# Two of the merge's sixteen column chunks projected among the last two heads of the first attention

## The chip, the cores and the metric

The kernel runs on one core of a Trainium2 chip. The metric is the device time of one execution in microseconds (us). The core has a matrix engine, TensorE (PE in the profile, its weight loads PEld), and four others: VectorE (DVE), ScalarE (ACT), GpSimd (POOL) and SyncE (SP). Each runs its own list of instructions in a fixed order; they meet at semaphores. DMA queues move data between the chip's memory and the core's own.

## What is computed

The reference is two transformer blocks. The change lies in the first attention part of the first one, for 512 tokens of width 1024. Of it this matters:

```python
z = u @ w_in[layer]
q_a, kc, vc, ksl, vsl, kwn, vwn, g_a, q_b, k_b, v_b, m_a, m_b = jnp.split(z, split_at, axis=-1)
...
y_a = nsa_attention(q_a, k_cmp, v_cmp, k_slc, vsl.reshape(kv_shape), k_win, vwn.reshape(kv_shape), g_nsa, rel_bias) @ w_up_nsa[layer]
y_b = stick_breaking_attention(q_b.reshape(sb_shape), k_b.reshape(sb_shape), v_b.reshape(sb_shape)) @ w_up_sb[layer]
mixed = (jax.nn.sigmoid(m_a) * y_a + jax.nn.sigmoid(m_b) * y_b) @ w_out[layer]
```

There are eight softmax heads (`nsa_attention`) and eight stick-breaking heads. `m_a` and `m_b` are 1024 columns of `u @ w_in` each and are needed only in the last line, the merge.

## The kernel before

`attention1` lays out the first attention part. Activations stand transposed, features on the 128 partitions and the 512 tokens along the free dimension. It projects keys, values and queries of the softmax heads, runs the eight `nsa_head` generators, then projects q, k and v of the stick-breaking heads and runs the eight `sb_head` generators; `merge1` follows.

A matrix product in full precision is made of three: weights and activations are split into a high part and a rest (line 117: ScalarE copies the high part, VectorE subtracts it), and `mm3` (lines 127 to 129) multiplies high by high, high by rest and rest by high. `gemm` loops it over the eight blocks of 128 input features, so a chunk of 128 output columns of `w_in` is 24 matmuls of 128x128 weights against 512 tokens, into a PSUM bank of the tag G, of which there are two.

`m_a` and `m_b` are columns 2840 to 4888 of `w_in`, 16 chunks, numbered 0 to 15. `project` loads 256 columns at a time, splits them and calls `gemm` for each chunk; `take_m` copies the bank with VectorE (line 1079). Chunks 0, 1 and 8 stay in the core in a tile `sg`; the other thirteen go through a tile `mo` of two buffers and a DMA that POOL issues (line 1083) into the array `md` in the chip's memory, from which `merge1` reads them back. The pool of `mo` opens when the pools of the softmax heads close and takes their space, so a copy into `mo` waits until these heads have ended.

A softmax head computes the scores against the 32 compressed keys (`Sc`, eight small matmuls, line 666) and against two sets of keys (line 693), each row's minimum and sum (VectorE, line 695, ScalarE, line 697), turns the probabilities with the matmul's transpose (line 536), splits them (line 170) and multiplies them by the values into one bank O (lines 544 and 546). `in_turn` starts a head while the one before it is still at its values. A stick-breaking head (lines 745 to 790) makes score products, an exponential and a logarithm on ScalarE (lines 761 to 763), a maximum and a split on VectorE (lines 764, 765) and POOL (line 766), sums over later keys with triangular and all-ones matmuls (lines 769 and 775), and multiplies by the values (line 788).

The order on each engine is not the order in which the program is written. A scheduler simulates the program when it is built and gives each engine's free time to instructions that could go then; earlier code has precedence, later code fills. The merge's chunks depend on nothing but `u` and the weights, so their matmuls fill TensorE's gaps among the heads, as far as banks and weight buffers are free. This order is fixed in the program.

Of the kernel before, what the change touches and what calls it, by code (L numbers as in the profile page):

```python
# [9 lines left out]
F32 = mybir.dt.float32  # L10
# [37 lines left out]
class Tiles:  # L48

    def __init__(self, tiles, n):  # L50
        self.tiles, self.n = tiles, n
# [21 lines left out]
class Kernel:  # L73
    def __init__(self, tc, a, out):
        self.tc, self.nc, self.a, self.out = tc, tc.nc, a, out
        self.exps, self.split_after = [], []

    def pool(self, name, side="left"):
        return self.tc.tile_pool(name=name, bufs=1, side=side, reuse_waits="tile")
# [574 lines left out]
    def nsa_head(self, h, qn, kd, vs, kdc, vsc, gates, parts, wk):  # L654

        nc = self.nc
        r0, g = 64 * (h % 2), h // 4
        QS = wk.tile([128, 512], F32R, name="QS", bufs=2)
        self.stack(QS, qn[:, h // 2], r0)
        band = self.band(h, wk)  # L660

        Sc = self.ps("S", 3)
        for r in range(4):
            qb = 3 - r
            for i in range(2):
                nc.tensor.matmul(Sc[:, r * 32:r * 32 + 32], QS[:, qb * 128:(qb + 1) * 128], kdc[i][:, g],
                                 start=(i == 0), stop=(i == 1))
        xc = wk.tile([128, 4, 32], F32, name="xc", bufs=2)
        nc.vector.memset(xc[:, :, 31:32], BIG)
        bv = band[:, 31:896]  # L670
        b3 = bass.AP(tensor=bv.tensor, offset=bv.offset, ap=[list(bv.ap[0]), [128, 4], [16, 31]])
        nc.vector.tensor_add(xc[:, :, :31], Sc[:, :128].rearrange("p (r c) -> p r c", r=4)[:, :, :31], b3)
        st = wk.tile([128, 4, 8], F32, name="st", bufs=2)
        nc.vector.tensor_reduce(st[:, 0, 0:4], xc[:, :, :31], axis=AX.X, op=OP.min)
        ec = wk.tile([128, 4, 32], F32, name="ec", bufs=2)
        nc.vector.tensor_sub(ec, xc, st[:, 0, 0:4].unsqueeze(2).to_broadcast([128, 4, 32]))
        nc.scalar.activation(ec, ec, AF.Exp, scale=-1.0)
        nc.vector.tensor_reduce(st[:, 1, 0:4], ec[:, :, :31], axis=AX.X, op=OP.add)
        nc.vector.tensor_scalar(st[:, 1, 0:4], st[:, 1, 0:4], 1e-30, None, op0=OP.max)
        nc.vector.reciprocal(st[:, 1, 0:4], st[:, 1, 0:4])  # L680
        nc.vector.tensor_mul(st[:, 1, 0:4], st[:, 1, 0:4], gates[:, 3, :, h])
        nc.vector.tensor_mul(ec[:, :, :31], ec[:, :, :31], st[:, 1, 0:4].unsqueeze(2).to_broadcast([128, 4, 31]))
        Ps = []
        for b in range(2):
            P = wk.tile([128, 1280], F32, name="P", bufs=3)
            Ps.append(P)
            mn, sm = st[:, 2, 4 * b:4 * b + 4], st[:, 3, 4 * b:4 * b + 4]
            for qb in range(4):
                n = (qb + 1) * 128
                x = P[:, ROW[qb]:ROW[qb] + n]  # L690
                ps = self.ps("S", 3)
                for i in range(2):
                    nc.tensor.matmul(ps[:, :n], QS[:, qb * 128:(qb + 1) * 128], kd[b][i][:, :n],
                                     start=(i == 0), stop=(i == 1))
                nc.vector.tensor_tensor_reduce(x, ps[:, :n], band[:, 384 - qb * 128:512], 1.0, 3e38,
                                               OP.add, OP.min, mn[:, qb:qb + 1])
                nc.scalar.activation(x, x, AF.Exp, bias=mn[:, qb:qb + 1], scale=-1.0, accum_out=sm[:, qb:qb + 1])
            yield
        Tc = self.ps("T", 2)
        for r in range(4):  # L700
            nc.tensor.transpose(Tc[:32, (3 - r) * 128:(4 - r) * 128], ec[:, r], self.ident)
        C = wk.tile([32, 512], F32, name="C", bufs=1)
        nc.scalar.activation(C, Tc[:32], AF.Copy)
        O = self.ps("O", 1)
        nc.tensor.matmul(O, vsc[:, g], C, start=True, stop=False, skip_group_check=True)
        for b in range(2):
            P, sm = Ps[b], st[:, 3, 4 * b:4 * b + 4]
            nc.vector.tensor_scalar(sm, sm, 1e-30, None, op0=OP.max)
            nc.vector.reciprocal(sm, sm)
            nc.vector.tensor_mul(sm, sm, gates[:, 1 + b, :, h])  # L710
            for qb in range(4):
                self.scale_rows(qb, P, sm)
            self.transposed_values(O, lambda j: vs[b][:, j, g], P, wk, False, b == 1)
            if b == 0:
                yield
        self.heads_parts(h, O, parts, self.np)
# [110 lines left out]
                self.gemm(ps, self.parts(w[:, :, m:m + 128]), [x[:, :, at] for x in act])  # L827
                consume((s + m) // 128, ps)

    def project(self, u, name, c0, n, consume, k0=0, first=None, k=8, early=(), banks=()):  # L830

        step = 2048 // k // 128 * 128
        done = 128 * len(early)
        if early:
            w = [self.load(self.w_cols(name, c0 + s, step, k0, k)) for s in range(0, done, step)]
            v = [self.parts(w[i // 2][:, :, i % 2 * 128:i % 2 * 128 + 128], place) for i, place in enumerate(early)]
            self.split_after = [self.normed]
            ps = [self.ps("S", 3) if i > 1 else self.ps("G", 2) for i in range(len(v))]  # L840
            for at in HALVES:
                for i, (x, y) in enumerate(zip(ps, v)):
                    self.gemm(x[:, at], y, [z[:, :, at] for z in u], after=self.behind_ms if i == 2 else None)
            for i, x in enumerate(ps):
                consume(i, x)
                self.step()
        for s in range(done // step * step, n, step):
            if s >= done:
                w = first[0] if first and s == 0 else self.load(self.w_cols(name, c0 + s, min(step, n - s), k0, k))
            else:  # L850
                w = w[-1]
            whole = self.parts(w) if k == 1 else None
            for m in range(max(0, done - s), min(step, n - s), 128):
                ps = self.ps(*banks[(s + m) // 128]) if (s + m) // 128 < len(banks) else self.ps("G", 2)
                e = min(m + 128, n - s)
                if whole:
                    v = [x[:, :, m:e] for x in whole]
                else:
                    v = first[1][m // 128] if first and first[1] and s == 0 else self.parts(w[:, :, m:e])
                self.gemm(ps[:e - m], v, u)  # L860
                consume((s + m) // 128, ps)
                self.step()

# [124 lines left out]
    def attention1(self, u, md, first, dram):  # L988

        nc = self.nc  # L990
# [5 lines left out]
        with self.pool("nsap") as sp:  # L996
# [4 lines left out]
            with self.pool("nsa0") as wk:  # L1001
# [36 lines left out]
                kdc, vsc = self.compress(sp, wk, kg[:, 0:1])  # L1038
# [13 lines left out]
            def keep(dst, scale):  # L1052
                def f(m, ps):
                    nc.scalar.activation(dst[:, m], ps, AF.Copy, scale=scale)
                return f
# [5 lines left out]
            self.project(u, "w_in", 1304, 512, keep(qT, 0.125))  # L1061
            self.project(u, "w_in", 1816, 512, keep(kT, 1.0))
            self.project_rows(u, "w_in", 2328, 512, take_vb)
        with self.pool("mo") as mw:
            self.sg = sbq.enter_context(self.pool("sg", "right"))
            with self.pool("sbw") as wk:

                self.in_turn([self.sb_head(h, qT, kT, vT, places.take, wk) for h in range(8)])


            self.kept = {}

            def take_m(first):
                def f(m, ps):
                    m += first
                    stay = m in (0, 1, 8)
                    t = self.sg.tile([128, 512], F32, name="sg", bufs=3) if stay else \
                        mw.tile([128, 512], F32, name="mo", bufs=2)
                    nc.vector.tensor_copy(t, ps)
                    if stay:  # L1080
                        self.kept[m] = t
                    else:
                        nc.gpsimd.dma_start(md[:, m * 512:(m + 1) * 512], t)
                return f

            for m, n in ((2, 6), (10, 6), (0, 2), (8, 2)):
                self.project(u, "w_in", 2840 + m * 128, n * 128, take_m(m))
        return places_a.new, places.new

# [912 lines left out]
```

## Time and profile before

| what | us |
|---|---|
| median of 3 runs (1799.74 to 1805.24) | 1800.09 |
| the profiled execution, its own time | 1800.61 |
| its span, from the first to the last instruction | 1798.9 |
| TensorE busy | 1719.1 (96%) |
| VectorE busy | 1393.7 (77%) |
| ScalarE busy | 1147.7 (64%) |
| POOL busy | 471.3 (26%) |

Busy times overlap, and an engine's busy share is a mean over stretches with different limits; the change touches the stretch from 228 to 457 us of the span. In a timeline, a bracket at the end of a row is the time in which the engine had nothing to run before that instruction and what ended the wait. The ends of matmuls are modelled and overlap the next one, so their cost is read from start to start. The granted clock is TensorE's, as a share of 2.4 GHz.

### The profile page before, as it was taken

How to read it: one execution, taken by the hardware profiler on the slowest of the kernel's cores; microseconds unless marked ns; L12 is line 12 of the kernel's file. 1: busy time of each engine (PE TensorE's matmuls, PEld its weight loads, DVE VectorE, ACT ScalarE, POOL GpSimd, SP SyncE). 2: the span in 40 equal slices, each digit the busy share in tenths (PEclk: the TensorE clock that was granted, in tenths of full speed). 3: DMA queues.
4: the chain of work that ended last, by engine and by line, in shares of the span. 5: the costliest groups of instructions: out<-in, count | busy, mean ns of one | idle time of the engine just before them, and what ended most of it. 6: DMA issues, size and time to landing. Idle time of an engine off the chain costs nothing. (4 is left out here: it accounts for less than half of the span.)

```text
span 1798.9 us, 24837 instructions
## 1 busy us (share of the span) xinstructions
PE 1719.1 (96%) x8944; PEld 1410.8 (78%) x8944; DVE 1393.7 (77%) x2022; ACT 1147.7 (64%) x1809; POOL 471.3 (26%) x433
## 2 busy tenths in 40 slices
PE   6899998999999999999999999969999999999996
PEld 2678976787898888888979888757777777777774
DVE  4758788888687474747765867879999989999997
ACT  3646676665565343435555666558888878888886
POOL 2204325435133333333312410221212112121113
PEclk9999999999999999999999999979999999999998
DMA  9634113315555656564522214679999999999954
GB/s 326 188 94 137 52 59 125 116 65 192 186 164 183 212 168 211 167 207 153 158 83 83 71 48 176 222 242 343 361 357 359 337 328 385 373 366 368 372 191 168
DMA packets 234400, 377.71 MB, mean 210 GB/s; under 512 B 11817, under 2 KB 102565, under 8 KB 234272
## 3 DMA queue, kind: packets, MB, share of 16 engines
q1 hardware_dynamic: 222752, 345.60, 56.1%
q0 software_dynamic: 11520, 30.47, 5.5%
q8 instruction: 72, 1.18, 0.3%
q14 instruction: 56, 0.46, 0.1%
HBM read 366.64 MB, written 20.73 MB: 215 GB/s over the span
## 5 line engine op out<-in xcount | busy, mean ns | idle before, releaser
L117 ACT ACTIVATE w<-raw 128x1024 fp32r<-128x1024 f32 (+2 forms) x350 | 353.5, 1017 | 296.1 <-PE G L128 226.7
L117 DVE TENSOR_TENSOR w<-raw,w 128x1024 fp32r<-128x1024 f32 (+2 forms) x350 | 422.1, 1225 | 114.4 <-ACT w L117 112.5
L127 PE MATMUL G<-u,w 128*128 128x512 f32 (+1 forms) x688 | 267.8, 390 | 7.7 <-ACT w L117 5.5
L128 PE MATMUL G<-u,w 128*128 128x512 f32 (+1 forms) x688 | 266.2, 387 | 0.4 <-DVE u L229 0.4
L129 PE MATMUL G<-u,w 128*128 128x512 f32 (+1 forms) x688 | 265.8, 387 | 0.1
L127 PE MATMUL S<-w,x 128*128 128x512 f32 x504 | 198.0, 398 | 6.4 <-PEq L1828 3.5
L128 PE MATMUL S<-w,x 128*128 128x512 f32 x504 | 202.7, 402 | 0.0
L129 PE MATMUL S<-w,x 128*128 128x512 f32 x504 | 199.9, 397 | 0.1
L117 DVE TENSOR_TENSOR w<-rawa,w 128x1024 fp32r<-128x1024 f32 x122 | 151.1, 1271 | 19.0 <-ACT w L117 19.0
L127 PEld LDWEIGHTS G<-u,w 128*128 128x128 f32 x688 | 130.6, 190 | 36.5 <-ACT w L117 6.2
L129 PEld LDWEIGHTS G<-u,w 128*128 128x128 f32 x688 | 130.8, 190 | 26.7 <-DVE w L117 2.1
L128 PEld LDWEIGHTS G<-u,w 128*128 128x128 f32 x688 | 131.0, 190 | 25.6 <-DVE u L229 1.0
L117 ACT ACTIVATE w<-rawa 128x1024 fp32r<-128x1024 f32 x122 | 127.9, 1060 | 35.7 <-PE S L129 21.9
L405 POOL TENSOR_TENSOR acc<-acc,araw 128x512 f32<-128x512 f32 x60 | 88.1, 1486 | 238.0 <-ACT araw L403 237.8
L127 PEld LDWEIGHTS S<-w,x 128*128 128x128 f32 x504 | 95.6, 190 | 29.7 <-issue 3.9
L129 PEld LDWEIGHTS S<-w,x 128*128 128x128 f32 x504 | 95.7, 190 | 22.2 <-POOL x L1683 0.9
L128 PEld LDWEIGHTS S<-w,x 128*128 128x128 f32 x504 | 95.8, 190 | 21.1
L128 PE MATMUL G<-hid,w 128*128 128x512 f32 (+1 forms) x320 | 111.1, 347 | 1.2 <-DVE hid L1120 1.2
L129 PE MATMUL G<-hid,w 128*128 128x512 f32 (+1 forms) x320 | 111.3, 348 | 0.0
L127 PE MATMUL G<-hid,w 128*128 128x512 f32 (+1 forms) x320 | 110.9, 347 | 0.0
L1683 POOL TENSOR_TENSOR x<-xg,x 128x512 fp32r<-128x512 f32 x32 | 47.5, 1486 | 228.2 <-ACT x L1682 228.2
L128 PE MATMUL G<-w,hh 128*128 128x512 f32 x248 | 100.8, 407 | 0.0
(637 smaller groups left out, 4021.7 us busy)
## 6 DMA issues: line engine op xcount, KB each, us to landing
raw<-in_mlp_w_dram SPq DMA_DIRECT2D x36, 1024.0 KB, 5.4
raw<-in_w_in_dram SPq DMA_DIRECT2D x33, 1024.0 KB, 5.3
raw<-in_w_expert_up_dram SPq DMA_DIRECT2D x28, 1024.0 KB, 10.0
raw<-in_w_expert_gate_dram SPq DMA_DIRECT2D x27, 1024.0 KB, 9.7
raw<-in_w_expert_down_dram SPq DMA_DIRECT2D x27, 1024.0 KB, 8.8
araw<-in_w_ada_dram SPq DMA_DIRECT2D x96, 256.0 KB, 3.6
rawa<-in_w_expert_gate_dram SPq DMA_DIRECT2D x21, 1024.0 KB, 10.9
rawa<-in_w_expert_up_dram SPq DMA_DIRECT2D x20, 1024.0 KB, 8.8
```

The source lines that it names most:

```text
L117: ins = nc.scalar.activation(r[0], v, AF.Copy), nc.vector.tensor_sub(r[1], v, r[0])
L127: first = nc.tensor.matmul(ps, lhs[0], rhs[0], start=start, stop=False)
L128: nc.tensor.matmul(ps, lhs[0], rhs[1], start=False, stop=False)
L129: self.behind = nc.tensor.matmul(ps, lhs[1], rhs[0], start=False, stop=stop)
L405: nc.gpsimd.tensor_add(x, x, raw)
L1683: nc.gpsimd.tensor_sub(x[1][:, s], y[:, s], x[0][:, s])
```

## The change

The last matmul of each softmax head's compressed scores is kept in a list, `marks`. While the softmax heads' pools are still open, chunks 2 and 3 are projected with a new consumer, `take_early`, which copies the bank into a tile `rstd` of the pool `np` (one buffer) and sends it to `md`. The first matmul of chunk 2 is ordered behind the mark of head 6, that of chunk 3 behind the mark of head 7. The later loop over the chunks begins with chunk 4 instead of chunk 2.

```diff
@@ nsa_head @@
             for i in range(2):
-                nc.tensor.matmul(Sc[:, r * 32:r * 32 + 32], QS[:, qb * 128:(qb + 1) * 128], kdc[i][:, g],
-                                 start=(i == 0), stop=(i == 1))
+                ins = nc.tensor.matmul(Sc[:, r * 32:r * 32 + 32], QS[:, qb * 128:(qb + 1) * 128], kdc[i][:, g],
+                                       start=(i == 0), stop=(i == 1))
+        self.marks.append(ins)
@@ project @@
-                self.gemm(ps[:e - m], v, u)
+                self.gemm(ps[:e - m], v, u, after=behind[(s + m) // 128] if behind else None)
@@ attention1 @@
+            def take_early(m, ps):
+                t = self.np.tile([128, 512], F32, name="rstd", bufs=1)
+                nc.vector.tensor_copy(t, ps)
+                nc.gpsimd.dma_start(md[:, (m + 2) * 512:(m + 3) * 512], t)
+
+
+            self.project(u, "w_in", 2840 + 256, 256, take_early, behind=self.marks[6:8])
         with self.pool("mo") as mw:
...
-            for m, n in ((2, 6), (10, 6), (0, 2), (8, 2)):
+            for m, n in ((4, 4), (10, 6), (0, 2), (8, 2)):
                 self.project(u, "w_in", 2840 + m * 128, n * 128, take_m(m))
```

The new order follows from the scheduler. In the rows below, `G<-u,w` is a chunk's matmul, `O<-P,vs` a value product of a softmax head, `T<-ident,P` a transpose, `O<-P,V` a value product of a stick-breaking head and `neg_tri`, `neg_ones_r` its sums over later keys; the numbers in names tell tiles apart. The lines of after are one higher from the mark on.

TensorE at head 6's second half, where its values meet the first set of probabilities; before:

```order
L536 MATMUL T<-ident,P 128x128 x4
L705 MATMUL O<-C,vsc 128x512
L544 MATMUL O<-P_2139,vs_624 128x512
L546 MATMUL O<-P_2140,vs_624 128x512
L544 MATMUL O<-P_2150,vs_624 128x384
L536 MATMUL T<-ident,P 128x128 x2
L546 MATMUL O<-P_2151,vs_624 128x384
```

and after, up to the first of the chunk matmuls that now stand there:

```order
L544 MATMUL O<-P_2139,vs_624 128x512
L536 MATMUL T<-ident,P 128x128 x2
L546 MATMUL O<-P_2140,vs_624 128x512
L536 MATMUL T<-ident,P 128x128 x3
L127 MATMUL G<-u_164,w_3851 128x512
L128 MATMUL G<-u_165,w_3851 128x512
L129 MATMUL G<-u_164,w_3852 128x512
```

Before, head 6's value products of 512 and 384 tokens follow each other directly; after, 21 chunk matmuls stand between them, the last of 72 behind head 7's mark.

VectorE at head 6's score reductions (ISA rows), before:

```order
L170 TENSOR_TENSOR P_1924<-T,P_1923 128x256
L682 TENSOR_TENSOR ec<-ec,st 128x4x31
L695 ISA P,st<-S,band 128x256
L695 ISA st 128x1
L695 ISA P,st<-S,band 128x384
L695 ISA st 128x1
L117 TENSOR_TENSOR w_3905<-raw,w_3904 128x1024
L695 ISA P,st<-S,band 128x512
```

and after:

```order
L170 TENSOR_TENSOR P_1913<-T,P_1912 128x512
L170 TENSOR_TENSOR P_1924<-T,P_1923 128x256
L696 ISA P,st<-S,band 128x384
L696 ISA st 128x1
L1068 COPY rstd<-G 128x512
L696 ISA P,st<-S,band 128x512
L696 ISA st 128x1
L117 TENSOR_TENSOR w_3852<-raw,w_3851 128x1024
```

The copy of chunk 2 out of its bank (line 1068) now stands between two score reductions, and the split of weights in this place is that of a later load.

TensorE in stick-breaking head 5, before:

```order
L127 MATMUL G<-u_164,w_4299 128x512
L128 MATMUL G<-u_165,w_4299 128x512
L129 MATMUL G<-u_164,w_4300 128x512
L788 MATMUL O<-P_3550,V 128x384
L788 MATMUL O<-P_3549,V 128x128
L788 MATMUL O<-P_3550,V 128x128
L769 MATMUL S<-s_3519,neg_tri 128x256
L775 MATMUL S<-s_3519,neg_ones_r 128x256
L775 MATMUL T<-s_3519,neg_ones_r 128x256
```

and after:

```order
L770 MATMUL T<-s_3600,neg_tri 128x512
L776 MATMUL T<-s_3599,neg_ones_r 128x384
L789 MATMUL O<-P_3629,V 128x384
L770 MATMUL S<-s_3599,neg_tri 128x256
L789 MATMUL O<-P_3630,V 128x384
L789 MATMUL O<-P_3629,V 128x128
L789 MATMUL O<-P_3630,V 128x128
L770 MATMUL S<-s_3600,neg_tri 128x384
L770 MATMUL S<-s_3599,neg_tri 128x128
```

Before, chunk matmuls stand between the head's value products; after, none is left from here to the end of the heads.

## Rows read from the trace of the kernel before

**Rows 1.** Span and mean granted TensorE clock of the core.

```profile
core 0: 1798.9 us, clock 0.983
```

**Rows 2.** Windows by stretch: start:end, length; busy us per engine (instructions); granted clock; DMA.

```profile
228.50:244.40 15.90, 15.90 (x91) 13.03 (x89) 11.04 (x28) 10.16 (x24) 1.97 (x3) 1.00 0.31 89
244.40:257.20 12.80, 12.61 (x78) 10.44 (x77) 12.39 (x43) 8.94 (x25) 4.86 (x8) 1.00 0.23 77
257.20:265.40 8.20, 7.67 (x47) 5.94 (x47) 7.75 (x31) 7.48 (x20) 1.88 (x4) 1.00 0.00 0
265.40:284.20 18.80, 14.99 (x87) 11.08 (x85) 12.64 (x31) 9.05 (x22) 3.79 (x6) 0.94 0.01 1
284.20:292.30 8.10, 8.06 (x26) 6.47 (x27) 7.98 (x8) 6.29 (x12) 7.22 (x6) 0.73 0.62 199
292.30:329.40 37.10, 33.26 (x159) 26.24 (x158) 34.01 (x41) 23.86 (x43) 22.36 (x18) 0.95 0.53 169
329.40:390.00 60.60, 59.22 (x319) 49.91 (x318) 49.95 (x75) 39.41 (x74) 23.06 (x22) 1.00 0.24 79
390.00:429.20 39.20, 38.57 (x207) 32.09 (x206) 31.54 (x55) 23.05 (x44) 17.40 (x16) 1.00 0.32 92
429.20:457.00 27.80, 23.82 (x102) 18.78 (x102) 22.52 (x29) 13.11 (x23) 14.40 (x20) 0.94 0.90 312
```

**Rows 3.** Windows by stretch, TensorE on tile G alone; same columns.

```profile
228.50:244.40 15.90, 9.28 (x36) 1.00 0.31 89
244.40:257.20 12.80, 4.00 (x14) 1.00 0.23 77
257.20:284.20 27.00, 0.00 (x0) 0.96 0.00 1
284.20:292.30 8.10, 8.06 (x26) 0.73 0.62 199
292.30:390.00 97.70, 63.01 (x244) 0.98 0.35 113
390.00:429.20 39.20, 25.76 (x100) 1.00 0.32 92
```

**Rows 4.** Windows, VectorE's weight splits (line 117) alone.

```profile
228.50:244.40 15.90, 3.38 (x3) 1.00 0.31 89
...
390.00:429.20 39.20, 3.96 (x5) 1.00 0.32 92
```

**Rows 5.** Windows, VectorE's copies of chunks (line 1079) alone, stick-breaking heads 5 to 7.

```profile
390.00:429.20 39.20, 2.75 (x4) 1.00 0.32 92
```

**Rows 6.** TensorE's timeline: start, duration, line, operation; [idle before <-releaser].

```profile
246.13 0.39 PE L127 MATMUL G<-u,w 128*128 128x512 f32 x1
246.36 0.39 PE L128 MATMUL G<-u,w 128*128 128x512 f32 x1
246.59 0.39 PE L129 MATMUL G<-u,w 128*128 128x512 f32 x1
...
263.77 1.12 PE L705 MATMUL O<-C,vsc 32*128 32x512 f32 x2 [0.49 <-DVE sq L522]
...
268.03 0.73 PE L693 MATMUL S<-kd,QS 128*128 128x512 f32 x2 [1.08 <-DVE st L695]
269.19 0.39 PE L546 MATMUL O<-P,vs 128*128 128x256 f32 x1 [0.43 <-DVE P L170]
...
284.24 0.79 PE L127 MATMUL G<-u,w 128*128 128x512 f32 x1 [1.01 <-DVE mo L1079]
284.83 0.63 PE L128 MATMUL G<-u,w 128*128 128x512 f32 x1
285.26 0.63 PE L129 MATMUL G<-u,w 128*128 128x512 f32 x1
```

**Rows 7.** Waits, 390.0 to 429.2: us in total, times, longest.

```profile
POOL s L766 <- DVE s L765: 17.1, 5, 5.2
...
DVE e L764 <- ACT e L763: 4.6, 2, 2.5
```

More of the change, by code (lines that the diff above doesn't have):

```diff
@@ L75, in __init__ @@
         self.tc, self.nc, self.a, self.out = tc, tc.nc, a, out
-        self.exps, self.split_after = [], []
+        self.exps, self.split_after, self.marks = [], [], []
     def pool(self, name, side="left"):
@@ L828, in project_half, with project @@
                 consume((s + m) // 128, ps)
-    def project(self, u, name, c0, n, consume, k0=0, first=None, k=8, early=(), banks=()):
+    def project(self, u, name, c0, n, consume, k0=0, first=None, k=8, early=(), banks=(), behind=()):
         step = 2048 // k // 128 * 128
```

## The prediction, made before the changed kernel ran

> **What bounds the kernel now.** I first read the clock and the span of the core [rows 1], then cut the region of the first attention part that the change touches, 228.5 to 457 us, at landmarks of the program and read every engine's busy time in each stretch [rows 2]. The landmarks: 228.5, the sixth softmax head (head 5) is under way; 244.4, head 6 has its last score product (line 666), the point behind which the change puts one chunk; 257.2, head 7 has its own, behind which it puts the other; 284.2, TensorE is done with the softmax heads; 292.3, the first of the eight stick-breaking heads is in full run; 390.0, the fifth of them ends; 429.2, the last one ends; 457, the merge is in full run. I call 228.5–244.4 A, 244.4–257.2 B, 257.2–284.2 C, 284.2–292.3 D.
>
> TensorE is what the region runs on: busy 15.90 of 15.90 in A, 12.61 of 12.80 in B, 59.22 of 60.6 and 38.57 of 39.2 in the two long stick-breaking stretches [rows 2]. It is so busy because chunk matmuls, which wait for little, stand wherever the heads would make it wait. Where no chunk stands, it waits: in the end of C (265.4–284.2) it is busy 14.99 of 18.80, with VectorE's results named at the waits [rows 2, 6]. VectorE is near its own limit in B, 12.39 of 12.80 [rows 2]. So each stretch has a TensorE time (heads plus chunks) and a VectorE time, and the larger sets its length.
>
> The chunk matmuls by stretch, counted in the order of before, are 34 in A, 14 in B, 0 in C, 26 in D, 243 in stick-breaking heads 0 to 4, 67 in heads 5 to 7, where 33 matmuls of the merge stand as well; the trace has 36, 14, 0, 26, 244 and 100 on the tile G (the 36 with two of an earlier projection) [rows 3]. One of them costs 0.23 us from start to start at 2.4 GHz (246.13, 246.36, 246.59) and 0.43 at 1.2 GHz (284.83, 285.26) [rows 6]. Their total is the same after; only their places change. So the sum below is a sum of idle time gained and lost on TensorE.
>
> **The change, stretch by stretch.** In the order of after, A has no chunk matmul, B 24, C 72, D 25, heads 0 to 4 have 263 and 10 of the merge, heads 5 to 7 none and 23 of the merge.
>
> A loses 34. TensorE alone would fall by 34 × 0.23 = 7.8. VectorE stands in the way: 11.04 busy, less one split of weights, which leaves the stretch, 3.38 / 3 = 1.1 [rows 2, 4], is 9.9; I add 0.9, twice what VectorE leaves idle in B, its fullest stretch (12.80 − 12.39). So A takes 10.8, **−5.1**. Ends: −7.8, and −3.5 if A takes the 12.4 that VectorE's work takes in B.
>
> B gains 10: 10 × 0.23 = **+2.3**. The low end is one more copy on VectorE, 2.75 / 4 = 0.7 [rows 5]; the high end both, 3.0. The early copy stands in VectorE's order between two score reductions, so the softmax behind it comes 0.7 later; TensorE has chunk work in its queue there, so I cost that at nothing beyond B's high end. The copy's DMA is issued by POOL, which is busy 4.86 of 12.80 in B [rows 2].
>
> C gains 72, all ahead of the second value product of head 6's second half (265.43 in before); the last 18.8 us of C get none. They cost 72 × 0.23 = 16.6. What they can cover is the waits that lie beside them or just behind: 0.49 at 263.77, 1.08 at 268.03, 0.43 at 269.19 [rows 6], 2.0 together. So **+14.6**. The later waits of C are not covered: there TensorE, ScalarE and VectorE pass head 7's blocks to each other, and those operations cannot start before head 6's values have left the one O bank. The high end is 16.6; the low end is the first rival.
>
> The busy time of TensorE in C is 7.67 + 14.99 = 22.7 of 27.0, which leaves 4.3 to fill, but the weight loads are busy only 5.94 + 11.08 = 17.0, which leaves 10.0 [rows 2]. The Trainium skill ("Trainium Kernel Development and Optimization", section "Performance Expectations") calls matmul busy time a bad measure of closeness to the limit, since matmuls are pipelined, and the busy share of weight loads a good one; by it C could take 10.0 us of chunks for nothing and would grow by 6.6 rather than 14.6.
>
> D and heads 0 to 4 gain 20 chunk matmuls less one, and 10 of the merge, 29 × 0.23 = **+6.7**. TensorE idles 3.8 in 292.3–329.4 and 1.4 in 329.4–390.0 [rows 2]; if a third of that takes some up it is +5.0, the low end. The stall at 284.24, where the first chunk of D waits for a bank that VectorE copies late, is the same in both orders, and so is the fall to 1.2 GHz around it (granted 0.73 in D) [rows 2, 6]: costed at nothing.
>
> Heads 5 to 7 lose 67 + 33 − 23 = 77. TensorE alone would fall by 77 × 0.23 = 17.7, to 21.5. VectorE has 31.54, less three copies (3 × 0.69 = 2.1) [rows 5] and three half splits (3 × 3.96 / 5 = 2.4) [rows 4], so 27.1. Without filling work the heads' own chain sets the pace: POOL waits 17.1 us for VectorE and VectorE 4.6 for ScalarE there already [rows 7]. VectorE was 92% busy in 292.3–329.4 (34.01 of 37.1), the stick-breaking stretch in which TensorE idled most, and 82% in the next [rows 2]. I take 27.1 / 0.92 = 29.5, **−9.7**; at 82% it is 33.0, −6.2, and with no gap at all 27.1, −12.1. Six small DMAs that now stand on POOL ahead of the last subtractions there lie inside POOL's waits.
>
> The merge (from 429.2) has the same matmuls left in both orders: 0.
>
> Sum: −5.1 + 2.3 + 14.6 + 6.7 − 9.7 = **+8.8**. Read as idle time: A saves 2.7 less than its matmuls cost, C hides 2.0, heads 5 to 7 save 8.0 less than theirs; 2.7 − 2.0 + 8.0 = 8.7. What is late after the change is TensorE in C, then VectorE's chain in the emptied heads. The profiled execution of before took 1800.61 us, its span is 1798.9, and the median of the runs is 1800.09, 0.5 lower; so 1800.6 + 8.8 − 0.5 = 1808.9, rounded to **1809**.
>
> **Rivals.**
>
> *The chunks hide in C (not slower).* C's end may be set by head 7's chain on VectorE, ScalarE and POOL, with TensorE a follower: then a front part of C that is longer lets VectorE and ScalarE run ahead, and the end of C shrinks. For it: weight loads leave 10.0 of C idle, and VectorE has only 20.4 of work in 27.0 [rows 2]. Against it: all 72 stand before the part with the waits, and what can be done ahead ends with three score banks and three buffers of probabilities. With all 10.0 covered C grows by 6.6 and the sum is +0.8, 1801. It decides against my forecast from 5.4 covered on, against the 2.0 I took. To be faster by over 0.3%, it would need A at −7.8, heads 5 to 7 at −12.1 and +5.0 in heads 0 to 4 as well: 6.6 − 7.8 + 2.3 + 5.0 − 12.1 = −6.0, 1794.
>
> *The clock falls in the emptied heads (slower still).* In 292.3–329.4, with TensorE 90% busy, the granted clock is 0.95 [rows 2]: a tenth of 37.1, 3.7 us, at 1.2 GHz, which costs half of that, 1.9. Heads 5 to 7 at 1.00 now would have about 21.5 of TensorE work in 29.5, so a fall to 1.2 GHz there, or two, is likely, but it costs only where TensorE is the last to come. Two of them in full are +3.8, so 1813. The Trainium skill ("TensorE: Matmul & The Clock Gate", section "Part 1: The HAM clock gate") says the throttled clock is the default and activity releases it; the fall at the thin end of C agrees (0.94 and then 0.73 [rows 2]).
>
> That the change does not do what it says is excluded by the order, which is fixed when the program is built.
>
> **How the numbers follow.** Two runs of this kernel can be told apart from about 0.3%, 5.4 us. My forecast has 0.60: its own range is 1804 (5.4 covered in C, +5.0 in heads 0 to 4: −5.1 + 2.3 + 11.2 + 5.0 − 9.7 = +3.7) to 1816 (all high ends: −3.5 + 3.0 + 16.6 + 6.7 − 6.2 = +16.6), of which 0.10 lies within 0.3% and 0.50 above. The first rival has 0.26, 0.18 within and 0.08 faster. The second has 0.14, slower. So faster 0.08, same 0.28, slower 0.64. The range reaches down to 1799, most of the first rival, and up to the same 1816, under which the second rival lies.
>
> **What would show it.** In the trace of after: from head 5 to head 6's score product 10.8 us, B 15.1, C 41.6 with TensorE busy nearly all of its first half and the same waits in its last 18 us, heads 5 to 7 29.5 with VectorE at some 92% and TensorE waiting. I am wrong if C is under 38 us, if heads 5 to 7 take under 27 or over 33, or if the merge starts with more or less left to do.

## The result: slower by 0.6 to 0.7%

The changed kernel took 1814.20 us (median of 6 runs, 1810.12 to 1816.39) beside 1799.91 us for the kernel before; the ratio is 1.0074 with a 95% interval of 1.0060 to 1.0088. Beside the first experiments it took 1811.39 (4 runs) against 1801.12, ratio 1.0060 [1.0043, 1.0077]. By these ratios it is slower by 11 to 13 us; the forecast was +8.8.

I measure both profiles between the same landmarks, read from the first and last rows of the named instructions: A from the end of head 5's line 666 products to those of head 6 (224.1 to 244.6 before, 223.2 to 236.4 after), B to those of head 7, C to the last value product of the softmax heads, then D with stick-breaking head 0, heads 1 to 4, 5, 6 and 7, each to its last value product, and the merge to the point where ScalarE starts on the eighth tile of its result. A begins 4.4 us earlier here than the A of the prediction. The windows of after, with the columns of [rows 2]:

```profile
223.20:236.40 13.20, 12.15 (x86) 10.59 (x86) 12.84 (x41) 11.30 (x28) 4.59 (x8) 1.00 0.34 101
236.40:252.70 16.30, 15.41 (x91) 12.76 (x91) 14.81 (x46) 10.37 (x28) 5.42 (x9) 1.00 0.33 98
252.70:274.40 21.70, 21.70 (x111) 17.70 (x111) 15.17 (x43) 11.49 (x29) 4.47 (x7) 1.00 0.13 43
274.40:291.90 17.50, 15.83 (x95) 12.30 (x93) 9.09 (x19) 7.24 (x14) 1.94 (x3) 1.00 0.07 24
...
401.80:410.80 9.00, 8.04 (x45) 6.09 (x45) 8.25 (x15) 4.52 (x11) 5.45 (x7) 1.00 0.51 144
410.80:424.70 13.90, 10.99 (x50) 8.59 (x50) 10.99 (x20) 7.11 (x15) 3.77 (x3) 0.69 0.23 71
424.70:437.70 13.00, 11.64 (x37) 9.05 (x36) 8.14 (x13) 6.78 (x11) 5.42 (x5) 0.54 0.45 136
437.70:490.80 53.10, 46.76 (x218) 37.95 (x219) 36.77 (x53) 27.63 (x45) 13.92 (x20) 0.90 0.58 191
```

The third row is the front of C: TensorE busy 21.70 of 21.70. The fourth is its thin end, 17.5 us, where before took 17.8 between the same landmarks (265.4 to 283.2). Heads 6 and 7 (the rows from 410.8 and 424.7) ran at a granted clock of 0.69 and 0.54. The kernel before, in the same heads and in the merge, between the same landmarks:

```profile
404.40:416.20 11.80, 11.80 (x73) 10.45 (x72) 10.91 (x21) 4.87 (x11) 3.52 (x3) 1.00 0.02 4
416.20:429.20 13.00, 12.68 (x60) 9.99 (x59) 9.46 (x16) 9.26 (x15) 9.40 (x10) 1.00 0.70 194
429.20:478.50 49.30, 45.32 (x219) 37.14 (x219) 38.88 (x55) 26.88 (x43) 14.94 (x21) 0.97 0.70 237
```

There the clock was at 1.00 in both heads, and head 7 did 60 matmuls in the 13.0 us in which it now does 37.

All stretches of all kernels, in us (from the timelines of each kernel's profiled run, to about 0.1; the names are those of the experiments below; time and ratio are the medians of the runs and their ratio to the kernel before, measured beside each):

| kernel | A | B | C | D, head 0 | 1 to 4 | 5 | 6 | 7 | merge | sum | time | ratio |
|---|---|---|---|---|---|---|---|---|---|---|---|---|
| before | 20.5 | 12.7 | 25.9 | 46.4 | 60.6 | 14.3 | 11.8 | 13.0 | 49.3 | 254.4 | | |
| after | 13.2 | 16.4 | 39.2 | 44.3 | 65.7 | 8.9 | 13.9 | 12.9 | 53.2 | 267.6 | 1814.2 | 1.0074 |
| after_again | 13.2 | 16.4 | 39.2 | 45.2 | 65.7 | 8.9 | 13.5 | 12.5 | 51.6 | 266.2 | 1811.4 | 1.0060 |
| x1_two | 13.2 | 16.4 | 29.8 | 44.9 | 60.0 | 14.3 | 11.8 | 12.8 | 49.5 | 252.6 | 1800.7 | 0.9997 |
| e2_free | 20.5 | 20.8 | 27.1 | 48.2 | 59.0 | 12.9 | 10.2 | 14.1 | 49.9 | 262.7 | 1809.6 | 1.0061 |
| e1_dup | 13.2 | 16.4 | 39.1 | 44.7 | 66.1 | 12.9 | 12.6 | 13.1 | 49.0 | 267.1 | 1814.1 | 1.0073 |
| e5_hold | 13.2 | 16.4 | 39.2 | 45.1 | 60.8 | 13.9 | 14.1 | 15.4 | 47.8 | 265.8 | 1812.9 | 1.0076 |
| e6_rep | 13.2 | 16.4 | 39.1 | 45.4 | 63.4 | 11.5 | 12.6 | 13.0 | 50.3 | 264.9 | 1809.6 | 1.0045 |
| v1_tail | 20.5 | 13.3 | 26.8 | 47.5 | 61.7 | 12.7 | 12.1 | 9.3 | 51.0 | 254.8 | 1802.9 | 1.0008 |
| v4_tail_hold | 20.5 | 13.2 | 26.8 | 48.0 | 59.0 | 12.5 | 14.2 | 15.7 | 48.6 | 258.6 | 1806.4 | 1.0033 |
| x4_tail_hold | 13.2 | 16.3 | 26.1 | 57.7 | 55.7 | 12.5 | 14.1 | 15.6 | 47.8 | 259.1 | 1806.2 | 1.0033 |
| y3_tail | 13.2 | 16.4 | 26.2 | 50.8 | 59.8 | 13.1 | 13.1 | 18.7 | 48.1 | 259.3 | 1809.1 | 1.0045 |
| y1_tail | 13.2 | 16.4 | 26.1 | 52.8 | 58.9 | 13.1 | 13.1 | 11.7 | 48.4 | 253.6 | 1803.1 | 1.0021 |

From before to after the softmax part (A to C) grows from 59.1 to 68.8, +9.7. Heads 5 to 7 return 3.4 of it, D to head 4 take 3.0 and the merge 3.9 more.

### The profile page after: what moved, and what is told of

It is laid out like the page before. It is cut to its first block, busy times and chain, and to the rows that moved or that the text cites. A ratio compares the mean times of both kernels' runs of the same rounds, so it can differ in the third digit from the quotient of the medians.

```text
span 1811.8 us, 24833 instructions
## 1 busy us (share of the span) xinstructions
PE 1726.7 (95%) x8944; PEld 1416.1 (78%) x8944; DVE 1395.0 (77%) x2022; ACT 1147.0 (63%) x1809; POOL 472.4 (26%) x433
## 3 DMA queue, kind: packets, MB, share of 16 engines
q1 hardware_dynamic: 222752, 345.60, 55.7%
## 5 line engine op out<-in xcount | busy, mean ns | idle before, releaser
L117 DVE TENSOR_TENSOR w<-rawa,w 128x1024 fp32r<-128x1024 f32 x122 | 151.1, 1271 | 20.1 <-ACT w L117 18.5
L128 PEld LDWEIGHTS G<-u,w 128*128 128x128 f32 x688 | 130.2, 189 | 26.1 <-DVE u L229 1.6
L127 PEld LDWEIGHTS S<-w,x 128*128 128x128 f32 x504 | 96.0, 190 | 29.7 <-issue 3.9
L1692 POOL TENSOR_TENSOR x<-xg,x 128x512 fp32r<-128x512 f32 x32 | 47.5, 1485 | 229.5 <-ACT x L1691 229.5
## 6 DMA issues: line engine op xcount, KB each, us to landing
raw<-in_w_expert_up_dram SPq DMA_DIRECT2D x28, 1024.0 KB, 11.8
```

The costliest lines, as they stand in the source:

```text
L117: ins = nc.scalar.activation(r[0], v, AF.Copy), nc.vector.tensor_sub(r[1], v, r[0])
L127: first = nc.tensor.matmul(ps, lhs[0], rhs[0], start=start, stop=False)
L128: nc.tensor.matmul(ps, lhs[0], rhs[1], start=False, stop=False)
L1692: nc.gpsimd.tensor_sub(x[1][:, s], y[:, s], x[0][:, s])
```

## The experiments

Three theories were at stake. **Theory 1**: filling work ran out in the last heads, TensorE's clock fell there, and this is where the time went. **Theory 2**, its rival: the heads' own chain on the other engines sets the late stretch, and the clock only follows. **Theory 3**, formed after the first four runs: the loss is made in C, and not by the two chunks that the change moves. Their early copies free the two PSUM banks, and chunks 4 and 5, which before had to wait for the end of the softmax heads, follow them in.

### The late stretch: after_again, e1_dup, e6_rep, e5_hold

> The changed kernel once more, beside the experiments on the same chip, for its spread and to see what of its late stretch repeats in a second profile. Both theories: 1810 to 1816; clock below 0.8 in heads 6 and 7.

It took 1811.39 us. Every stretch repeats within 0.5 us but D with head 0 (0.9) and the merge (1.6). Its heads 6 and 7:

```profile
411.90:425.40 13.50, 10.75 (x50) 8.87 (x50) 10.78 (x20) 7.11 (x15) 3.37 (x3) 0.75 0.24 74
425.40:437.90 12.50, 9.76 (x37) 7.33 (x35) 8.07 (x14) 6.88 (x11) 5.80 (x5) 0.73 0.47 140
```

This is the same program with the same 50 and 37 matmuls, but the granted clock is 0.75 and 0.73 where it was 0.69 and 0.54. Each head is 0.4 us shorter. So the clock weighs little in those parts of the heads in which the two profiles differ by it.

The second run does the two chunks twice.

```diff
-            for m, n in ((4, 4), (10, 6), (0, 2), (8, 2)):
+            for m, n in ((2, 6), (10, 6), (0, 2), (8, 2)):
```

> Edit: the changed kernel, but chunks 2 and 3 are projected a second time in the loop among the stick-breaking heads (48 matmuls with their weight load, splits and two copies more than needed; they overwrite the same values). Theory 1 (the late heads and the merge's start lost time because filling work ran out there and TensorE fell to 1.2 GHz: 35.8 us for heads 5 to 7 and +4.5 in the merge): the extra work lies where TensorE was slow or waiting, so 48 x 0.23 = 11 us of it come nearly free: 1814 +- 3, granted clock of 410 to 440 us near 1.0. Theory 2 (the heads' own chain and the work of the other engines set the late stretch, the clock only follows; TensorE is the limit earlier): the extra matmuls are paid, 1820 to 1825.

It took 1814.12 us, against 1811.39 for the changed kernel on the same chip: 48 more matmuls, 11 us at 0.23 each, cost 2.7. TensorE has that much room after C. Theory 2 as it was put, with the extra work paid, missed. The run does not show that the clock made the room: time in which TensorE waits for other engines would take the matmuls in as well. Heads 5 to 7 took 38.6 us instead of 34.9, the merge 2.6 less.

The third adds matmuls alone, in one product of the merge.

```diff
+                    v = self.parts(wu[i][:, :, m:m + 128])
+                    if k == 0 and i == 0:
+                        for j in [5, 6]:
+                            self.gemm(py, v, os_[i], after=self.sbm[j])
-                    self.gemm(py, self.parts(wu[i][:, :, m:m + 128]), os_[i])
+                    self.gemm(py, v, os_[i])
```

(`sbm` holds the last score sum of each stick-breaking head.)

> Edit: the changed kernel, with the first product of the merge (12 matmuls) computed three times over in its bank, the second and third time behind the last score sum of stick-breaking heads 5 and 6: 24 useless matmuls, nothing for any other engine. It measures the clock by itself. Theory 1: TensorE stays at 2.4 GHz longer, heads 6 and 7 get no longer (26.9 us in the changed kernel) in spite of 24 x 0.23 = 5.5 us more work, 1810 to 1814. Theory 2: the clock does not matter for the end; the matmuls are hidden (1814) or paid (up to 1820).

It took 1809.57 us (1808.29 to 1810.46), against 1811.02 to 1813.24 for the changed kernel: with 24 useless matmuls it is 1.8 us faster, in four runs of each. Its windows over heads 5, 6 and 7:

```profile
399.50:411.00 11.50, 9.97 (x55) 7.73 (x54) 9.74 (x18) 6.06 (x15) 7.62 (x10) 1.00 0.17 39
411.00:423.60 12.60, 12.60 (x75) 10.83 (x74) 9.75 (x17) 7.05 (x15) 3.02 (x2) 1.00 0.13 43
423.60:436.60 13.00, 9.60 (x36) 7.01 (x35) 8.93 (x15) 6.86 (x11) 4.56 (x4) 0.74 0.57 173
```

Head 6 has 75 matmuls at a clock of 1.00 and takes 12.6 us; in the changed kernel it had 50 at 0.69 and took 13.9. That does not show the low clock as the cause in head 6. The heads share the work out anew: VectorE is busy 9.75 in head 6 here and 10.99 there, ten matmuls of the merge moved from heads 1 to 4 into head 5, and head 5 takes 11.5 instead of 8.9. Head 7, at 0.74, takes 13.0. Heads 5 to 7 together take 37.1, against 35.7 and 34.9 in the two profiles of the changed kernel; what is shorter are heads 1 to 4 (63.4 against 65.7) and the merge (50.3 against 53.2 and 51.6). So the useless matmuls are hidden, as in e1_dup, and Theory 1's reason for it is not shown.

The fourth holds work back for the last heads.

```diff
+            hold = {0: [3, 4], 8: [5, 6]}
             for m, n in ((4, 4), (10, 6), (0, 2), (8, 2)):
-                self.project(u, "w_in", 2840 + m * 128, n * 128, take_m(m))
+                self.project(u, "w_in", 2840 + m * 128, n * 128, take_m(m), behind=[self.sbm[i] if i is not None else None for i in hold[m]] if m in hold else ())
```

> Edit: the changed kernel, but the last four chunks are held back: the first matmul of chunks 0, 1, 8 and 9 is ordered behind the last score sum of stick-breaking heads 3, 4, 5 and 6, so that each of the heads 3 to 6 has 24 chunk matmuls and heads 6 and 7 have 15 and 18 of the merge as well (the changed kernel: 47, 38, 0, 0 chunk matmuls, and 10, 8, 3, 12 of the merge in heads 4 to 7). No work is added or removed. Theory 1: the clock stays at 2.4 GHz in heads 5 to 7 and the merge's start is as before, -4 to -8 against the changed kernel: 1806 to 1810. Theory 2: heads 3 and 4 lose what heads 5 and 6 gain, and the merge stays late: 1813 to 1816.

It took 1812.94 us (1809.80 to 1818.36), no better than the changed kernel: Theory 1 missed. In its profiled run, the fastest of the four, heads 1 to 4 save 4.9 and the merge 3.8 to 5.4, but heads 5 to 7 grow by 7.7, from 35.7 to 43.4, at clocks of 0.83, 1.00 and 0.78. Work moved into the last heads is paid there too. And the 9.7 of A to C stand untouched in all four runs, so the softmax part had to be looked at.

### Where the loss is made: x1_two, e2_free

The marks for these runs: `vm` holds the last value product of each of a softmax head's six steps, so that `vm[47]` is the end of head 7, and `late` gives each chunk what its first matmul is ordered behind.

```diff
+            late = {4: self.vm[47], 5: self.vm[47]}
             for m, n in ((4, 4), (10, 6), (0, 2), (8, 2)):
-                self.project(u, "w_in", 2840 + m * 128, n * 128, take_m(m))
+                self.project(u, "w_in", 2840 + m * 128, n * 128, take_m(m), behind=[late.get(m + i) for i in range(n)])
```

> Edit: the changed kernel, but the first matmuls of chunks 4 and 5 are ordered behind head 7's last value product. So just the two chunks of the change stand among the last softmax heads: 24 matmuls in B, 24 in C instead of 72, and from the stick-breaking heads on the places are those of before (74 against 69 up to the first value product, then 24, 36, 37, 36, 37, 34, 24 and 9 with 33 of the merge, against 18, 46, 37, 36, 37, 34, 24 and 9 with 33). Theory 3 (the loss is the 48 matmuls of chunks 4 and 5, which can enter C because the early copies free the two banks, 48 x 0.23 = 11 us, of which the late heads give only some 7 us back): C grows by 2.3 instead of 13.3, the softmax part from head 5's scores on by -7.3 + 3.6 + 2.3 = -1.4 instead of +9.6, the rest as before: 1797 to 1801. Rival (the two chunks themselves, with copies and splits on a full VectorE, cost their time there): the softmax part still grows by 5 or more, 1805 to 1810.

It took 1800.70 us against 1801.00, ratio 0.9997 [0.9986, 1.0008]: no difference from the kernel before. The two chunks are where the change puts them, A and B are those of the changed kernel to a tenth, and C is 29.8 instead of 39.2. Its window of C:

```profile
252.60:282.30 29.70, 27.08 (x156) 20.95 (x156) 21.45 (x58) 16.39 (x41) 6.42 (x10) 1.00 0.03 10
```

C has 156 matmuls on record where the changed kernel has 111 + 95 = 206. The 48 matmuls of chunks 4 and 5 cost 39.2 − 29.8 = 9.4 us in C, 0.2 each, so nearly all of them are paid. The softmax part is 59.4, as before 59.1. This is Theory 3, and it is shown: holding two chunks back that the change does not mention takes the whole loss away. Not all of it lies in C, though. The sums of the two kernels differ by 15.0: 9.4 in C, and 5.6 behind it, although the changed kernel has 48 chunk matmuls fewer to do there. Early work that is paid in C would be no loss if the later stretches gave its price back; they do not (heads 1 to 4 are 5.7 longer, the merge 3.7, heads 5 to 7 3.2 shorter).

The counterpart keeps the early exit and drops the marks.

```diff
-            self.project(u, "w_in", 2840 + 256, 256, take_early, behind=self.marks[6:8])
+            self.project(u, "w_in", 2840 + 256, 256, take_early)
```

> Edit: the changed kernel without the order behind the marks: chunks 2 and 3 leave early, but their matmuls go where there is room. A gets 34, B 50, C 12 instead of 0, 24 and 72; all in all 96 as in the changed kernel, and heads 5 to 7 get 13, 0 and 0 with 18, 3 and 21 of the merge. Theory 3 (the freed banks let chunks 4 and 5 in, 48 matmuls more than before among the softmax heads, whatever the marks say): the softmax part grows by 8 to 11 us, 1807 to 1813. Rival (it is the place behind heads 6 and 7 that costs): the softmax part grows by less than 4, 1800 to 1804.

It took 1809.60 us, ratio 1.0061 [1.0041, 1.0080]. A is that of before, B takes 20.8 instead of 12.7, and the softmax part 68.4, +9.3. With the chunks in another place the loss is the same. It depends on how many matmuls get in, not on the marks.

### Other places for the chunks: v1_tail, v4_tail_hold, x4_tail_hold, y3_tail, y1_tail

The thin end of C [rows 2] is the one stretch where TensorE visibly waits. These kernels put a chunk there, three matmuls at a time behind single value products; v1_tail and v4_tail_hold chunk 4, the others chunk 3.

```diff
-            if after and k == 0:
+            if isinstance(after, list):
+                self.order(first, after[k])
+            elif after and k == 0:
                 self.order(first, after)
...
+            late = {4: [self.vm[i] for i in (36, 37, 39, 40, 42, 43, 45, 46)], 5: self.vm[47]}
```

> Edit: chunks 2 and 3 leave their banks early as in the changed kernel, but without order behind marks, so that their matmuls stand where they stood before (34 in A, 14 in B); the eight groups of three matmuls of chunk 4 are ordered one by one behind value products of heads 6 and 7, and chunk 5 behind the last one. So the thin end of C, where TensorE is busy 15.0 of 18.8 us, gets 24 matmuls, singly. Theory 3: they fill waits and keep the clock up there, the softmax part grows by 0 to 2 us and 24 matmuls less are left for later: -2 to -5, 1796 to 1799. Rival (chunk matmuls among the last heads are paid wherever they stand): the softmax part grows by 5.5, the late heads give half of it back: 1803 to 1806.

It took 1802.88 us, ratio 1.0008 [0.9997, 1.0019]. That lies between the two expectations, at the edge of the rival's. Half of what I expected came: 22 of the 24 matmuls are on record in C now, and C takes 0.9 us more (26.8 against 25.9). But it gave nothing back: D with head 0 takes 1.1 more, heads 1 to 4 1.1 more and the merge 1.7, and what head 5 and 7 gain (5.3) only levels that. Head 7 is worth a look. It has 12 matmuls of the merge and none of a chunk, as in the changed kernel; its window:

```profile
418.50:427.80 9.30, 6.92 (x27) 5.15 (x26) 6.44 (x11) 6.01 (x10) 3.21 (x2) 0.82 0.42 127
```

At a clock of 0.82 it takes 9.3 us, in the changed kernel at 0.54 13.0. The two windows do not hold the same work: some of head 7's own matmuls already stand in head 6 here (27 on record in the window against 37, VectorE busy 6.44 against 8.14). What can be compared are the twelve matmuls of the merge, which stand ahead of the last three value products in both. In the changed kernel, then here:

```profile
432.34 0.80 PE L127 MATMUL G<-qn,w 128*128 128x512 f32 x1
...
437.14 0.51 PE L789 MATMUL O<-P,V 128*128 128x384 f32 x3
```

```profile
423.85 0.79 PE L127 MATMUL G<-qn,w 128*128 128x512 f32 x1
...
427.29 0.50 PE L794 MATMUL O<-P,V 128*128 128x384 f32 x3
```

They take 4.80 and 3.44 us, so 1.4 of the 3.6 is the clock.

> Edit: as v1_tail, and chunks 8 and 9 are held behind the last score sums of stick-breaking heads 5 and 6 (24 chunk matmuls in head 6, and 15 and 18 of the merge in heads 6 and 7, instead of 3, 21 and 12). Theory 1 (filling work is worth more in the last heads than in the ones before them): 1 to 3 us under v1_tail. Rival: what heads 4 and 5 lose the last two gain, the same as v1_tail within 1.5 us, as with e5_hold.

It took 1806.42 us, 3.5 above v1_tail. Neither side had that: heads 1 to 5 gave up 2.9 us, and heads 6 and 7 grew by 8.5 (21.4 to 29.9).

> Edit: the changed kernel, but chunk 3's eight groups of three matmuls are ordered one by one behind value products of heads 6 and 7, chunks 4 and 5 behind the last one, and chunks 8 and 9 held as in v4_tail_hold. A is empty as in the changed kernel, B has chunk 2, the thin end of C chunk 3. Theory 3: A -7.3, B +3.6, C 0 to +2, so the softmax part is 2 to 4 us shorter than before and the rest about as before: 1796 to 1799. Rival (paid wherever they stand): 1800 to 1803.

It took 1806.19 us, above both expectations. The softmax part is 55.6, 3.5 shorter than before, as expected; but D with head 0 takes 57.7 instead of 46.4, and the hold makes heads 6 and 7 29.7 again.

> Edit: as x1_two, but chunk 3's eight groups of three matmuls are ordered one by one behind value products of heads 6 and 7 (the thin end of C), and chunk 7 behind the last score sum of stick-breaking head 0, so that head 0 gets fewer chunk matmuls and heads 6 and 7 more (30, and 19 with 33 of the merge). In x4_tail_hold the same placement in A to C took 55.6 us against 59.1 before and 59.4 in x1_two; what was lost there came with 98 chunk matmuls in head 0 (50.0 us) and the hold in heads 5 to 7. Theory 3 (what counts is the idle time filled; a place among the heads costs 0.23 us a matmul where TensorE is full): the softmax part -3.5, the rest as before: 1796 to 1799. Rival (the late stretch takes it back): 1800 to 1804.

```diff
+            late = {4: self.vm[47], 5: self.vm[47], 7: self.sbm[0]}
```

It took 1809.14 us, above both ranges; the rival had the direction, not the size. The softmax part keeps its gain (55.8), but D with head 0 takes 50.8 although it has fewer matmuls than before (176 on record in it, against 186), and head 7, with 52, 18.7. The view of TensorE's waits from 278.4 to 329.1, D and head 0, names the engine waited for:

```profile
PE S L773 <- DVE s L769: 10.1, 3, 4.7
```

and VectorE's and POOL's timelines around the longest one:

```profile
308.73 6.36 DVE L769 CAST s<-e 128x256 fp32r<-128x256 f32 x3
...
309.88 0.66 POOL L1097 DMA_DIRECT2D md<-mo  x1
310.55 2.36 POOL L415 TENSOR_TENSOR acc<-acc,acc 128x1024 f32<-128x1024 f32 x1
312.86 1.94 POOL L770 TENSOR_TENSOR s<-e,s 128x256 fp32r<-128x256 f32 x2
```

The first of the three casts is 128x256, the others are 128x512; one of these takes 0.42 and the last 4.76, while POOL adds and subtracts without a pause. In x1_two, where D with head 0 takes 44.9, the three last 3.41 together (309.48), and TensorE waits 1.3 us for casts of this line; in x4_tail_hold and y1_tail it is 6.3 and 7.5, named as above.

> Edit: as y3_tail, but instead of chunk 7 it is chunk 10 that is ordered behind stick-breaking head 0's last score sum: head 0 gets 84 and 18 chunk matmuls instead of 57 and 12, heads 6 and 7 get 25 with 5 of the merge and 28 of the merge instead of 30 and 19 with 33. Theory 3: within 2 us of y3_tail if head 0's extra 33 matmuls cost 0.23 us each and are saved later. Rival (VectorE and POOL are the limit in head 0, which took 50 us in x4_tail_hold): 2 to 5 us above y3_tail.

It took 1803.10 us, ratio 1.0021 [1.0011, 1.0031], 6 below y3_tail and outside both expectations. D with head 0 grows by 2.0 only for 33 more matmuls, and head 7, now with the merge's 28 alone, takes 11.7 instead of 18.7. No version beats the kernel before; x1_two and v1_tail equal it within their intervals.

## Why the prediction was right, and where it was not

The sign was right and the measured times lie in its range; the size was low by 2 to 5 us. That the sum came so near is partly luck: A to head 4 were forecast at +18.5 and came at +12.7 and +13.5, heads 5 to 7 with the merge at −9.7 and came at +0.5 and −1.9, and the two errors offset each other. Step by step, the terms against the differences of the table (after, after_again):

| step | predicted | measured |
|---|---|---|
| A | −5.1 | −7.3, −7.3 |
| B | +2.3 | +3.7, +3.7 |
| C | +14.6 | +13.3, +13.2 |
| D and heads 0 to 4 | +6.7 | +3.0, +3.9 |
| heads 5 to 7 | −9.7 | −3.4, −4.2 |
| merge | 0 | +3.9, +2.3 |
| sum | +8.8 | +13.2, +11.8 |

**A and B.** VectorE is nearly full in A, 12.84 of 13.20, as forecast. But more of its work than one split left A; its busy time there fell from 15.55 to 12.84 between the landmarks, and rose in B from 12.32 to 14.81. Taken together the two were forecast at −2.8 and came at −3.6.

**C.** The step that carries the verdict held: 72 matmuls ahead of the thin end, nearly all paid, the thin end as long as before. The first rival, that they hide in idle weight loads, needed 5.4 us covered; 16.6 − 13.3 = 3.3 were, and weight loads are busy 17.70 + 12.30 = 30.0 of 39.2 now. By the busy share of weight loads, as the Trainium skill ("Trainium Kernel Development and Optimization", section "Performance Expectations") would have it, C would have grown by 6.6; the trace does not agree here: in the front of C TensorE is busy 21.70 of 21.70 with weight loads at 17.70, and most of the idle weight loads of before lay in the thin end (11.08 of 18.80 [rows 2]), where no chunk matmul stands. What the prediction did not say is that two thirds of this term are chunks 4 and 5, not the chunks that the change names. It had the count, 72, and did not ask where 48 of them came from.

**Heads 5 to 7** are the step that failed: they take 35.7 and 34.9 where 29.5 was forecast, over the 33 that the prediction gave as a sign of being wrong. VectorE's work was forecast at 27.1 and is 8.25 + 10.99 + 8.14 = 27.4; its share was forecast at 92% and is 27.4 / 35.7 = 77%. Head 5 did as forecast (9.0 us, VectorE 8.25, 92%), heads 6 and 7 did not. I took the share from 292.3–329.4 [rows 2], and its 34.01 us of busy VectorE are in part waiting: ten instructions there are drawn out beside POOL (a 128x512 cast among them takes 2.62 us, elsewhere 0.41), by some 9.8 us in all, an estimate that sets each against the shorter ones of its kind. Without them that stretch is at 65%, and the changed heads 5 to 7, with 5.3 less counted the same way, at 62%. So a high share did not mean that VectorE was the limit there; that this is the whole reason is not shown.

The second rival, two falls of the clock for 3.8, happened in the trace: 0.69 and 0.54. Its price was not. The same program at 0.75 and 0.73 is 0.8 shorter in the two heads, and the twelve merge matmuls in head 7 cost 1.4 more than at v1_tail's clock. No run divides up the rest of the 5.4 to 6.2 us over the forecast; it stays open.

**D and heads 0 to 4** took the 29 matmuls for 3.0 to 3.9 instead of 6.7. They all stand in heads 1 to 4, which paid 5.1, 0.18 each; D with head 0 has as many matmuls as before and came out 1.2 to 2.1 shorter, which I had not forecast; its clock was 0.96 where before had 0.90.

**The merge** at 0 was wrong. The same matmuls were left, but it meets head 7's output bare. TensorE's timeline of after, around the merge's first product that needs head 7:

```profile
442.82 0.79 PE L127 MATMUL G<-qT,w 128*128 128x512 f32 x2 [2.32 <-ACT qT L170]
447.16 0.80 PE L128 MATMUL G<-kT,w 128*128 128x512 f32 x1 [3.54 <-DVE kT L170]
```

It waits 2.3 us for ScalarE's and then 3.5 for VectorE's half of one split, with nothing in its order to run ahead. The product at 447.16 comes 9.5 us after head 7's end; before, its counterpart comes 5.7 after (434.96). So the first tile is 3.1 us later than before, 3.0 in after_again, near the 3.6 by which the split is longer (its cause is looked at in the last section); in after_again some of it is made up by the eighth tile. The two profiles differ by the clock: from 447.2 on the matmuls run at 0.43, in after until 453.6, in after_again until 450.7. Three us more at half speed make 1.5 of the 1.6 between them.

## What to carry to other kernels

When an edit gives a resource back earlier (a bank, a buffer), count what else enters through it, in the new order, before costing the work that the edit names: here the named work cost nothing and the work behind it 9 us, which the later stretches did not give back. Work moved off a stretch returns its full price only where that engine was the limit there; ask for each stretch which engine is next, and at which clock. In stretches that an edit empties, do not take the next engine's busy share from another stretch before looking at what its instructions do there: part of the share can be waiting. And do not price a low clock by the clock alone: it costs where matmuls stand back to back with something waiting behind them (1.4 us in head 7), and next to nothing where TensorE waits anyway.

## What the runs showed of the hardware

An instruction on VectorE can take six times its usual time beside POOL. The split of head 7's output takes 0.69 us in the profile of before (432.85) and in e6_rep (442.57); in the changed kernel it takes 4.30, in both of its profiles, while POOL issues three DMAs and adds a 128x1024 tile:

```profile
442.81 4.30 DVE L170 TENSOR_TENSOR kT<-sq,qT 128x512 fp32r<-128x512 f32 x1 [0.69 <-ACT qT L170]
...
442.56 1.62 POOL L975 DMA_DIRECT2D sg<-md  x3
444.19 2.35 POOL L413 TENSOR_TENSOR acc<-acc,acc 128x1024 f32<-128x1024 f32 x1
```

It ends 0.6 us after POOL does (447.11, against 446.54). The same split stands in all thirteen profiles. In five it meets no addition or subtraction on POOL and takes 0.68 or 0.69 (before, x1_two, e6_rep, y3_tail, y1_tail). In six it meets one and takes 1.36 to 1.76; in e5_hold it starts at 444.78 beside one from 444.38 to 445.66 and takes 1.42. In these six and in both profiles of the changed kernel it ends 0.5 to 0.6 us after POOL's instruction, near its own 0.69: it waits for POOL and then does its work. A copy that reads a PSUM bank is not drawn out: in y3_tail `mo<-G` at 306.74 takes 0.67 beside an addition on POOL that begins at 306.45 and lasts 1.28.

The Trainium skill ("GPSIMD Engine Reference", section "1. Specifications") says that POOL's interfaces to the core's memory (SBUF) are shared with VectorE, with contention for VectorE's instructions that have two inputs in this memory or run in a two-port mode. The split has two such inputs, so the rows agree. Whether POOL's DMA issues hold VectorE up too stays open (the split starts 1.4 us before the addition and is not done when that begins; a cast of 0.42 beside the DMA issue at 309.88 in y3_tail is not held), as does why D with head 0 grew in the kernels that filled the thin end of C.
